# Gate and norm of the decode rows apart from the main rows, and the decode steps spread anew over the projection phase

## The chip, the cores and the metric

The kernel runs on one core of one Trainium2 chip. The metric is the device time of one execution in microseconds; the time of before is the median of three runs. The engines that the text speaks of are TensorE (PE; PEld is its weight load), VectorE (DVE), ScalarE (ACT), GpSimd (POOL) and SyncE (SP), the last of which only issues transfers. ACT and POOL have transfer queues of their own too.

## What is computed

One layer of a decoder, on 1024 prompt positions (the main rows) and 8 decode rows of one position each, side by side as 1032 columns. Cut to the part that the change touches:

```python
proj = rmsnorm(x, norm1_w) @ w_in                 # z (1536) | x, B, C (2048) | dt (24 heads) | v (512)
xbc = silu(causal_dwconv(xbc, conv_state, conv_w, conv_b))
dt = softplus(dt_raw + dt_bias); a = -exp(a_log)
# main rows: the scan over 8 chunks of 128 positions, 24 heads of 64, 4 groups of B and C, state 64
# decode rows, for each head: one step of the same scan
h_new = exp(dt * a) * h + (dt * x) B              # (8 rows, 24, 64, 64): an output
y = sum_n(h_new * C) + d_skip * x
# both kinds of row
y = y * silu(z)
y = rmsnorm over each of 4 groups of 384 channels, times ssd_norm_w
x = x + concat(y, pooling(v)) @ w_out             # then the feed-forward part
```

All values are 32-bit floats. Each large product is made as three TensorE products of high and low parts: weight high with data high, weight high with data low, weight low with data high.

## The kernel before

Channels lie on the 128 partitions, positions along the free axis. `hn` holds eight row blocks of the normed input as high and low parts (`hh`, `hl`). A tile of `w_in` is 128 output channels; `gemm` makes it in three column chunks of 344, 24 products each, into a bank tagged `g`. `load_tile` loads the weights in two halves on SP's queue, and `weight_parts` (L140, L141) lets ACT make the high and a second engine, `lo_eng`, the low half; four half tiles (`wop`) are kept. `lo_eng` is POOL for tiles 1 to 5, 13, 15 and 6 to 9, and DVE from then on.

The order of the projection phase (`project`, `ssd_phase`):

- `startup` loads the input, norms it by column chunk (`norm`) and makes tiles 12 (B of the first two groups), 14 (C) and 0. `norm` lets DVE scale a row block, ACT make its high part and DVE (POOL for some) its low part; the list `low` says how many scaled blocks may wait for their low part. `dt_chain` makes dt, the decay tables of the scan and, for the decode rows, `dtS` (dt of each channel's head by row) and its decay `dA`.
- The tiles of x go through the convolution (`conv_tile`, `conv_close`: one tap on ACT, three on DVE, L516) and get their SiLU one tile later.
- The scan of one half of the heads (6 tiles of x, `q` = 0 and 1: the first and the second group of tasks) is a list of tasks, `queue`, from which `between` takes about two per tile before a column chunk of a running tile. For a chunk `c`, `decay` makes `mix` and `ce` (DVE L538, ACT, then POOL L553), `turn` the transposed inputs (L571 to L583), `apply` the chunk's state `h` (POOL L606, DVE L610) and its output (PE L620 and L630, DVE L638). The second group's tasks run beside gate tiles 0 to 6.
- `gate_tile(i)` makes z of tile i; a later hook, `gate`, has ACT take its SiLU and DVE multiply it in (L698 main rows, L700 decode rows). After each third gate `group_norm` squares and adds, `group_scale` takes the mean over the channels by a product with a matrix of ones (L721), rsqrt as exp(-0.5 ln) on ACT, and scales on DVE (L730).
- `sample_tile(i)` is the decode step of tile i: POOL loads the state `st` and, for some i, B and C broadcast to all partitions (`bc`, L662, from a small DRAM tensor `bcd` that `sample_bc` writes), then makes the new state, stores it, and adds up y over the 64 state entries in six halvings (L680). Its result is written over the tile's x of the decode rows, which L700 waits for.
- Steps 0 to 2 are queued between the two groups, 3 to 6 beside chunks 0, 2, 4 and 6 of the second. Gates 7 to 11, each with its own step ahead of it, come after the scan, and four pooling tiles (`pool_tile`: running sums on DVE L858, `mh` and `ml` as the parts for a small product) end the phase. `w_out` follows, whose first operands are `yh` and `yl`.

`issue_after` (in `behind`) puts an instruction behind another of the same engine; `self.pl` is the last state product L606, behind which the steps beside the scan are put. ACT holds one table set at a time: SiLU is in one set, exp and ln in the other; `tables` chains all such activations in the order of the code and loads a set where it changes. All else is ordered by a scheduler that runs when the program is built: it takes instructions by the order of the code and by when, on its own estimate of the engines' times, their inputs and buffers are there. On the chip each engine then keeps that order.

## Time and profile before

| | us |
|---|---|
| median of 3 runs (lowest, highest) | 1403.73 (1402.88, 1408.87) |
| profiled execution (its span) | 1407.76 (1406.0) |
| PE busy | 1360.4 (97%) |
| DVE, ACT, POOL busy | 991.2, 700.6, 561.5 |

The profile is of one execution. Times are counted from the start of its span. L12 is line 12 of the kernel before. Each row of a timeline gives the start, the length, the engine, line and operation, and in brackets how long the engine stood idle before it and which instruction ended that wait. The granted clock is a share of TensorE's full 2.4 GHz; its lower level, 1.2 GHz, is 0.50. The projection phase lasts until about 516 us, the output projection until about 715 us; the rest is the feed-forward part.

### The profile page before, as it was taken

The page shows a single profiled execution, that of the slowest core. Times are in us where ns is not written, and L with a number is a line of the kernel's source. Part 1 is how long each engine was busy: PE and PEld are TensorE (multiplying, and loading weights), DVE is VectorE, ACT ScalarE, POOL GpSimd, SP SyncE. Part 2 cuts the span into 40 slices and gives each one's busy share as a digit, 9 for nine tenths or more (in the row PEclk, how much of TensorE's full clock was granted, in tenths as well). Part 3 has the DMA queues.
Part 4 walks back from the last instruction along what each step waited for, and adds up shares of the span by engine and source line. Part 5 has one row for each costly group of instructions (what it writes and reads, how often), then busy time and mean ns, then how long its engine had stood idle before and what let it go on. Part 6 is the DMA issues. An engine that isn't in the chain of part 4 may idle for free. (4 is left out here: it accounts for less than half of the span.)

```text
span 1406.0 us, 26779 instructions
## 1 busy us (share of the span) xinstructions
PE 1360.4 (97%) x10360; PEld 1312.9 (93%) x10360; DVE 991.2 (70%) x1453; ACT 700.6 (50%) x1408; POOL 561.5 (40%) x704
## 2 busy tenths in 40 slices
PE   8999999979999999999979999999999999999997
PEld 7799879968799999899979999999999999999997
DVE  6575898669865684844689877777776787567743
ACT  6346774546644451311456545554554465444452
POOL 4233465888668305774222212212222224214122
PEclk9999999989999999999999999999999999999999
DMA  6031235243331256675477877777777769657513
GB/s 248 1 108 38 93 118 168 81 142 116 94 104 62 74 192 209 214 253 178 152 204 148 210 205 193 187 207 183 185 187 201 196 207 328 225 185 235 180 55 121
DMA packets 117820, 228.09 MB, mean 162 GB/s; under 512 B 19884, under 2 KB 37116, under 8 KB 117692
## 3 DMA queue, kind: packets, MB, share of 16 engines
q1 hardware_dynamic: 73772, 130.21, 29.3%
q0 software_dynamic: 27056, 70.22, 19.8%
q10 hardware_dynamic: 16864, 25.95, 5.6%
q8 instruction: 81, 1.33, 0.4%
q14 instruction: 47, 0.39, 0.1%
HBM read 169.64 MB, written 45.15 MB: 153 GB/s over the span
## 5 line engine op out<-in xcount | busy, mean ns | idle before, releaser
L1118 PE MATMUL g<-op,wop 128*128 128x258 f32 x3696 | 446.9, 283 | 4.3 <-DVE op L1048 1.6
L1118 PEld LDWEIGHTS g<-op,wop 128*128 128x128 f32 x3696 | 445.3, 189 | 5.6 <-DVE op L1048 2.0
L140 ACT ACTIVATE wop<-raw 128x512 fp32r<-128x512 f32 (+1 forms) x208 | 125.9, 608 | 231.2 <-PE g L161 139.7
L1300 PE MATMUL g<-op,wop 128*128 128x258 f32 x1848 | 224.9, 283 | 1.6 <-ACT op L210 0.9
L159 PE MATMUL g<-hh,wop 128*128 128x344 f32 x696 | 226.1, 325 | 0.0
L160 PE MATMUL g<-hl,wop 128*128 128x344 f32 x696 | 225.3, 324 | 0.0
L1300 PEld LDWEIGHTS g<-op,wop 128*128 128x128 f32 x1848 | 222.5, 189 | 2.7 <-ACT op L210 1.1
L161 PE MATMUL g<-hh,wop 128*128 128x344 f32 x696 | 224.8, 323 | 0.0
L141 DVE TENSOR_TENSOR wop<-raw,wop 128x512 fp32r<-128x512 f32 (+1 forms) x186 | 159.7, 862 | 83.3 <-ACT wop L140 81.5
L140 ACT ACTIVATE wop<-s 128x512 fp32r<-128x512 f32 (+1 forms) x136 | 83.6, 620 | 137.6 <-PE g L1300 51.9
L1098 POOL DMA_DIRECT2D s<-s x44 | 37.7, 857 | 249.8 <-DVE wop L141 89.2
L159 PEld LDWEIGHTS g<-hh,wop 128*128 128x128 f32 x696 | 132.2, 190 | 1.2 <-issue 1.1
L161 PEld LDWEIGHTS g<-hh,wop 128*128 128x128 f32 x696 | 132.1, 190 | 1.2 <-issue 1.2
L160 PEld LDWEIGHTS g<-hl,wop 128*128 128x128 f32 x696 | 132.1, 190 | 0.5 <-issue 0.4
L1200 DVE SCALAR_TENSOR_TENSOR acc<-u,cst,acc 128x1048 f32<-128x1048 f32 x88 | 115.2, 1309 | 12.2 <-ACT acc L1198 10.6
L141 DVE TENSOR_TENSOR wop<-s,wop 128x512 fp32r<-128x512 f32 (+1 forms) x136 | 92.1, 682 | 36.5 <-ACT wop L140 34.1
L1178 DVE TENSOR_TENSOR u<-u,g 128x258 f32<-128x258 f32 (+2 forms) x176 | 58.0, 354 | 72.2 <-PE g L1118 67.6
L1175 ACT ACTIVATE u<-g 128x258 f32<-128x258 f32 (+2 forms) x220 | 69.6, 340 | 71.2 <-PE g L1118 71.2
L160 PE MATMUL g<-yl,wop 128*128 128x344 f32 x288 | 93.4, 325 | 3.2 <-DVE yl L211 3.2
L161 PE MATMUL g<-yh,wop 128*128 128x344 f32 x288 | 93.0, 323 | 0.0
L159 PE MATMUL g<-yh,wop 128*128 128x344 f32 x288 | 92.9, 323 | 0.0
L1270 POOL DMA_DIRECT2D g<-td x77 | 41.2, 539 | 123.1 <-DVE op L211 70.2
(276 smaller groups left out, 2333.9 us busy)
## 6 DMA issues: line engine op xcount, KB each, us to landing
s<-wup SPq DMA_DIRECT2D x88, 256.0 KB, 3.2
g<-td POOLq DMA_DIRECT2D x77, 258.0 KB, 4.5
raw<-wup SPq DMA_DIRECT2D x66, 256.0 KB, 4.1
raw<-win SPq DMA_DIRECT2D x58, 256.0 KB, 2.7
mix<-acd SPq DMA_DIRECT2D x16, 768.0 KB, 4.5
td<-acc ACTq DMA_DIRECT2D x22, 516.0 KB, 6.1
s<-wup POOLq DMA_DIRECT2D x44, 256.0 KB, 5.3
s<-s POOLq DMA_DIRECT2D x44, 256.0 KB, 3.9
```

The costliest lines, as they stand in the source:

```text
L140: self.nc.scalar.activation(hi, raw[:, :w], AF.Copy)
L141: lo_eng.tensor_tensor(out=lo, in0=raw[:, :w], in1=hi.bitcast(F32), op=ALU.subtract)
L159: nc.tensor.matmul(ps[:, :n], wh, xh[:, sl], start=(first and k == 0), stop=False)
L160: nc.tensor.matmul(ps[:, :n], wh, xl[:, sl], start=False, stop=False)
L161: nc.tensor.matmul(ps[:, :n], wl, xh[:, sl], start=False, stop=(final and k == last))
L1098: nc.gpsimd.dma_start(t, raw[acc] if acc in raw else w[acc][j], accum_op=ALU.add)
L1118: nc.tensor.matmul(out, a, b, start=(p in OPENS and j == 1), stop=(j == 12), skip_group_check=True)
L1175: a = nc.scalar.activation(out, ps[:, s], AF.Copy, scale=-1.0 if p in ("p5", "p4") else 1.0)
L1178: nc.vector.tensor_tensor(out=out, in0=out, in1=ps[:, s], op=op)
L1200: nc.vector.scalar_tensor_tensor(out=acc, in0=u[:, k : k + FW], scalar=self.c("fw", 3 * n + k), in1=acc, op0=ALU.mult, op1=ALU.add)
L1270: self.loaded = self.nc.gpsimd.dma_start(st[:, j], self.td[i + j][ROW[p]]).ins
L1300: self.pe = nc.tensor.matmul(out, a, b, start=(s == 0 and i == 0 and j == 0), stop=(s == len(PIECES) - 1 and i == nk - 1 and j == 2),).ins
```

## The change

- Gate and norm of the decode rows are taken out of `gate`, `group_norm` and `group_scale`, which then handle the 1024 main columns only. ACT puts SiLU of the decode columns of z into a small tile `zs`. A new function, `group_decode(g)`, makes gate, squares, mean (three products with the matrix of ones, 8 columns each) and scale for the decode rows of one group of three tiles. It is called for group 0 after gate tile 9, for group 1 after gate tile 11, for groups 2 and 3 after the last two pooling tiles.
- Decode steps 0 and 1 are made after tiles 1 and 2 of x, ahead of the first group's chunks; steps 2 to 4 beside chunks 2, 4 and 6 of the second group; steps 5 to 8 before gates 7 to 10; steps 9 to 11 after gate 11. The last three take their buffers from the tag `pf`, in pairs. B and C are broadcast for steps 0, 2, 3, 5, 6 and 9 (before: 0, 3, 6, 7 and 9). `sample_bc` is called after tile 1 for the first half, and in the first group's chunk 2 for the second.
- `dtS` comes from a transfer of dt to DRAM and two broadcast loads of it, on POOL's queue, and not from two TensorE products; the matrices for these go from the constants.
- In `norm` of the first column chunk one scaled block may wait for its low part, not two.

```diff
@@ -69,8 +69,8 @@
 NCONST = _n
 
 
-M_ID, M_TRI, M_SEL, M_RM = 0, 128, 256, 384
-NMAT = 384 + 12
+M_ID, M_TRI = 0, 128
+NMAT = 256
 
 
 class Kernel:
@@ -321,7 +321,7 @@
                     if also is not None and k == 0:
                         with self.behind(act):
                             also()
-                    while low and (len(low) > 2 or k == KT - 1):
+                    while low and (len(low) > min(c + 1, 2) or k == KT - 1):
                         j, xj = low.pop(0)
                         hi, lo = self.hn[j]
                         eng = nc.gpsimd if j == 2 or (j == 5 and c > 0) else nc.vector
@@ -411,6 +411,12 @@
         nc.vector.tensor_tensor(out=l, in0=l, in1=q, op=ALU.add)
         self.dt = self.const.tile([P, n9], F32, name="dt")
         nc.vector.scalar_tensor_tensor(out=self.dt, in0=t, scalar=0.0, in1=l, op0=ALU.max, op1=ALU.add)
+
+        dtd = self.dram.tile([NH, NB], F32, name="dtd")
+        nc.gpsimd.dma_start(dtd.rearrange("h b -> b h"), self.dt[:NB, n8:n9])
+        self.dtS = self.const.tile([P, XT, NB], F32, name="dtS")
+        for g in range(2):
+            nc.gpsimd.dma_start(self.dtS[64 * g : 64 * g + 64], dtd[g::2].partition_broadcast(64))
         ea = cut(4 * n9, NH)
         self.tables(ea, self.c("alr", 0, NH), AF.Exp)
         dta = q[:, :n8]
@@ -447,23 +453,6 @@
         nc.sync.dma_start(
             self.acd.rearrange("c (h l) -> h c l", h=NH), rows[:NH, :].rearrange("h (c l) -> h c l", l=P)
         )
-
-        tp = self.bank("pM")
-        nc.tensor.transpose(tp[:NH, :NB], self.dt[:NB, n8:n9], self.mat[:NB, M_ID : M_ID + NB])
-        dts = cut(4 * n9 + NH, NB)
-        nc.vector.tensor_copy(dts[:NH], tp[:NH, :NB])
-        r = cut(900, XT * NB).rearrange("p (i b) -> p i b", b=NB)
-        nc.vector.tensor_tensor(
-            out=r[:NH], in0=self.mat[:NH, M_RM : M_RM + XT].unsqueeze(2).broadcast_to([NH, XT, NB]),
-            in1=dts[:NH].unsqueeze(1).broadcast_to([NH, XT, NB]), op=ALU.mult,
-        )
-        tp = self.bank("pT")
-        nc.tensor.matmul(
-            tp[:, : XT * NB], self.mat[:NH, M_SEL : M_SEL + P], r[:NH].rearrange("h i b -> h (i b)"),
-            start=True, stop=True,
-        )
-        self.dtS = self.const.tile([P, XT, NB], F32, name="dtS")
-        nc.vector.tensor_copy(self.dtS.rearrange("p i b -> p (i b)"), tp[:, : XT * NB])
         ec = cut(1000, XT)
         self.tables(ec, self.c("alc", 0, XT), AF.Exp)
         self.dA = self.const.tile([P, XT, NB], F32, name="dA")
@@ -655,17 +644,20 @@
         nc, d = self.nc, self.d
         g = (i // 3) % 2
         mk = lambda s, shape: self.ph.tile(shape, F32, tag=self.tags[s][0], name=self.nm(s), bufs=self.tags[s][1])
-        if i % 3 == 0 or i == 7:
+        if i % 3 == 0 or i in (2, 5):
             self.bc = mk("bc", [P, 2, NB, NST])
             for j in range(2):
                 src = self.bcd[q : q + 1, :, j * P + g * NST : j * P + (g + 1) * NST]
                 nc.gpsimd.dma_start(self.bc[:, j], src.rearrange("o b n -> (o b) n").partition_broadcast(P))
         bb, cc = self.bc[:, 0], self.bc[:, 1]
         xt = self.xs_samp(self.xs[i])
-        st = mk("st", [P, NB, NST])
+        if self.tags["st"] is None:
+            pair = self.ph.tile([P, 2, NB, NST], F32, tag="pf", name=self.nm("st"), bufs=2)
+            st, tmp = pair[:, 0], pair[:, 1]
+        else:
+            st, tmp = mk("st", [P, NB, NST]), mk("stt", [P, NB, NST])
         nc.gpsimd.dma_start(st, d["st_ssm"][i])
         dx = mk("dx", [P, 2, NB])
-        tmp = mk("stt", [P, NB, NST])
         bcast = lambda a: a.unsqueeze(2).broadcast_to([P, NB, NST])
         nc.gpsimd.tensor_tensor(out=dx[:, 0], in0=self.dtS[:, i, :], in1=xt, op=ALU.mult)
         nc.gpsimd.tensor_tensor(out=tmp, in0=bb, in1=bcast(dx[:, 0]), op=ALU.mult)
@@ -694,10 +686,9 @@
 
         def gate():
             z = box[0]
-            self.tables(z, z, AF.Silu)
+            self.tables(z[:, :SEQ], z[:, :SEQ], AF.Silu)
+            self.tables(self.zs[:, i], z[:, SEQ:TOK], AF.Silu)
             nc.vector.tensor_tensor(out=y[:, :SEQ], in0=y[:, :SEQ], in1=z[:, :SEQ], op=ALU.mult)
-            ys = self.xs_samp(y)
-            nc.vector.tensor_tensor(out=ys, in0=ys, in1=z[:, SEQ:TOK], op=ALU.mult)
             if i % 3 == 2:
                 self.group_norm(i // 3)
 
@@ -706,36 +697,52 @@
 
     def group_norm(self, g):
         nc = self.nc
-        sq = [self.short(SW, "sq") for _ in range(2)]
-        nc.scalar.activation(sq[0], self.xs[3 * g], AF.Square)
+        sq = [self.short(SEQ, "sq") for _ in range(2)]
+        nc.scalar.activation(sq[0], self.xs[3 * g][:, :SEQ], AF.Square)
         for i in range(1, 3):
-            nc.scalar.activation(sq[1], self.xs[3 * g + i], AF.Square)
+            nc.scalar.activation(sq[1], self.xs[3 * g + i][:, :SEQ], AF.Square)
             eng = nc.gpsimd if g < 2 else nc.vector
             eng.tensor_tensor(out=sq[0], in0=sq[0], in1=sq[1], op=ALU.add)
         self.later(2, lambda: self.group_scale(g, sq))
 
     def group_scale(self, g, sq):
         nc = self.nc
-        for j, (o, w) in enumerate(((0, 512), (512, 512), (1024, 32))):
-            pb = self.bank(("pT", "pY")[j % 2])
-            nc.tensor.matmul(pb[:, :w], self.ones, sq[0][:, o : o + w], start=True, stop=True)
-            self.tables(sq[1][:, o : o + w], pb[:, :w], AF.Ln, bias=self.eps, scale=1.0 / 384.0)
+        for j in range(2):
+            pb = self.bank(("pT", "pY")[j])
+            part = slice(j * 512, (j + 1) * 512)
+            nc.tensor.matmul(pb, self.ones, sq[0][:, part], start=True, stop=True)
+            self.tables(sq[1][:, part], pb, AF.Ln, bias=self.eps, scale=1.0 / 384.0)
         self.tables(sq[1], sq[1], AF.Exp, scale=-0.5)
-        for i in range(3):
-            y = self.xs[3 * g + i]
-            for o, a, r in (
-                (y[:, :SEQ], y[:, :SEQ], sq[1][:, :SEQ]),
-                (y[:, SEQ:TOK], self.xs_samp(y), self.xs_samp(sq[1])),
-            ):
-                nc.vector.scalar_tensor_tensor(
-                    out=o, in0=a, scalar=self.c("nw", 3 * g + i), in1=r, op0=ALU.mult, op1=ALU.mult
-                )
+        for i in range(3 * g, 3 * g + 3):
+            y = self.xs[i][:, :SEQ]
+            nc.vector.scalar_tensor_tensor(
+                out=y, in0=y, scalar=self.c("nw", i), in1=sq[1], op0=ALU.mult, op1=ALU.mult
+            )
+
+    def group_decode(self, g):
+
+        nc = self.nc
+        pb = self.bank("pT")
+        for i in range(3 * g, 3 * g + 3):
+            rows, s = self.xs[i][:, SEQ:TOK], self.zs[:, XT + i % 3]
+            nc.vector.tensor_tensor(out=rows, in0=self.xs_samp(self.xs[i]), in1=self.zs[:, i], op=ALU.mult)
+            nc.vector.tensor_tensor(out=s, in0=rows, in1=rows, op=ALU.mult)
+            nc.tensor.matmul(pb[:, :NB], self.ones, s, start=(i % 3 == 0), stop=(i % 3 == 2))
+        r = self.zs[:, XT + 3]
+        self.rsqrt(r, pb[:, :NB], 1.0 / 384.0)
+        for i in range(3 * g, 3 * g + 3):
+            rows = self.xs[i][:, SEQ:TOK]
+            nc.vector.scalar_tensor_tensor(
+                out=rows, in0=rows, scalar=self.c("nw", i), in1=r, op0=ALU.mult, op1=ALU.mult
+            )
 
     def project(self):
 
         nc, d, tc = self.nc, self.d, self.tc
         self.bcd = self.dram.tile([2, NB, 2 * P], F32, name="bcd")
         self.xs, self.bt, self.ctl = [None] * XT, {}, {}
+
+        self.zs = self.const.tile([P, XT + 4, NB], F32, name="zs")
 
         with ExitStack() as outer:
             with self.banks(g=3, pT=2, pY=2, pM=1) as self.ps:
@@ -745,10 +752,17 @@
                     self.ssd_phase()
             with self.banks(g=4, pT=2, pY=1, pM=1) as self.ps, tc.tile_pool(name="mix", bufs=1) as self.ph:
 
-                self.tags = {"bc": ("v", 2), "st": ("mh", 1), "stt": ("ml", 1), "dx": ("vs", 2)}
+                self.tags = {"bc": ("pf", 2), "st": ("mh", 1), "stt": ("ml", 1), "dx": ("vs", 2)}
                 for i in range(7, 12):
+                    if i < 11:
+                        self.sample_tile((i - 2) // 6, i - 2)
+                    self.gate_tile(16 + i, i, None)
+                    if i == 9:
+                        self.group_decode(0)
+                self.group_decode(1)
+                self.tags["st"] = None
+                for i in range(9, 12):
                     self.sample_tile(1, i)
-                    self.gate_tile(16 + i, i, None)
                 self.pool_groups()
 
     def ssd_phase(self):
@@ -784,10 +798,10 @@
                     trn[c + 1] = self.turn(q, c + 1, dec[c + 1][0])
                 if c + 2 < NCH:
                     dec[c + 2] = self.decay(q, c + 2)
-                if c == -1 and q == 0:
-                    self.sample_bc(q)
-                if q == 1 and c in (0, 2, 4, 6):
-                    sample(3 + c // 2)
+                if (q, c) == (0, 2):
+                    self.sample_bc(1)
+                if q == 1 and c in (2, 4, 6):
+                    sample(1 + c // 2)
 
             queue.append(start)
             for c in range(-1, NCH):
@@ -800,15 +814,16 @@
         self.lo_eng = nc.gpsimd
         for n in range(1, 6):
             self.keep(n, self.conv_tile(n, n, None))
+            if n == 1:
+                self.sample_bc(0)
+            if n < 3:
+                sample(n - 1)
         ssd_tasks(0)
         credit[:] = 0.35, 0.6
         for n in (13, 15, 6, 7, 8, 9):
             self.keep(n, self.conv_tile(n, n, between))
         flush()
         self.lo_eng = nc.vector
-        self.sample_bc(1)
-        for i in range(3):
-            queue.append(lambda i=i: sample(i))
         credit[1] = 0.7
         for n in (10, 11):
             self.keep(n, self.conv_tile(n, n, between))
@@ -887,6 +902,8 @@
         pf = {}
         for g in (3, 2, 1, 0):
             pf[g] = self.pool_tile(g, g == 0)
+            if g < 2:
+                self.group_decode(3 - g)
         self.hn = None
         self.w_out([pf[g] for g in range(4)])
 
@@ -1513,8 +1530,6 @@
     s, t = np.arange(P)[:, None], np.arange(P)[None, :]
     m[:, M_ID : M_ID + P] = s == t
     m[:, M_TRI : M_TRI + P] = s <= t
-    m[:, M_SEL : M_SEL + P] = (s % 2) == (t // 64)
-    m[:, M_RM : M_RM + XT] = (s // 2) == np.arange(XT)[None, :]
     return m
 
 
```

## Rows read from the trace of the kernel before

**Rows 1.** The page, first part: busy us of each engine, share, instructions.

```profile
PE 1360.4 (97%) x10360; PEld 1312.9 (93%) x10360; DVE 991.2 (70%) x1453; ACT 700.6 (50%) x1408; POOL 561.5 (40%) x704
```

**Rows 2.** Waits of PE, whole span: us in total, times, longest us.

```profile
PE pY L630 <- POOL ce L553: 9.8, 2, 9.2
...
PE pM L565 <- DVE h L610: 3.7, 4, 1.9
...
PE pY L620 <- DVE mix L583: 2.9, 2, 2.1
...
PE g L160 <- DVE hl L329: 2.6, 2, 2.3
```

**Rows 3.** Stretches: busy us by engine, granted clock, DMA share, GB/s.

```profile
core 0: us, PE busy (x) PEld busy (x) DVE busy (x) ACT busy (x) POOL busy (x), PEclk, DMA share, GB/s
95.00:135.00 40.00, 40.00 (x257) 39.30 (x256) 25.19 (x23) 21.97 (x34) 15.67 (x19) 1.00 0.18 55
...
143.00:219.00 76.00, 71.88 (x644) 61.55 (x641) 73.27 (x104) 52.82 (x116) 45.48 (x33) 0.98 0.37 118
...
310.00:397.00 87.00, 80.69 (x672) 70.15 (x671) 76.64 (x107) 56.16 (x114) 64.76 (x58) 0.96 0.34 109
397.00:471.00 74.00, 74.00 (x458) 72.08 (x458) 39.77 (x39) 35.59 (x52) 60.17 (x81) 1.00 0.26 82
...
471.00:505.00 34.00, 34.00 (x211) 33.01 (x210) 26.04 (x36) 14.75 (x32) 1.02 (x4) 1.00 0.26 74
```

**Rows 4.** Timelines of ACT, POOL and PE round the longest wait.

```profile
279.37 0.83 ACT L188 ACTIVATE ce<-ce 128x768 f32<-128x768 f32 x1
...
280.53 1.84 POOL L662 DMA_DIRECT2D bc<-bcd  x2
...
286.69 1.83 POOL L671 TENSOR_TENSOR stt<-bc,dx 128x512 f32<-128x512 f32 x1 [2.15 <-DMA bc<-bcd]
...
293.24 1.03 POOL L672 TENSOR_TENSOR st<-st,dA 128x512 f32<-128x512 f32 x1 [2.45 <-DMA st<-st_ssm]
294.24 1.79 POOL L553 TENSOR_TENSOR ce<-ce,xs 128x768 f32<-128x768 f32 x1
...
296.08 1.33 PE L630 MATMUL pY<-ce,h 64*64 64x128 f32 x10 [9.19 <-POOL ce L553]
```

**Rows 5.** Stretches of 10 us round that wait, columns as in rows 3.

```profile
290.00:300.00 10.00, 3.92 (x21) 2.82 (x23) 0.86 (x3) 2.00 (x6) 7.41 (x9) 0.50 0.17 52
300.00:310.00 10.00, 10.00 (x72) 9.08 (x69) 8.57 (x13) 1.78 (x4) 9.00 (x13) 0.85 0.51 146
```

**Rows 6.** Timelines of DVE and PE in the first column chunk.

```profile
11.79 2.58 DVE L313 SCALAR_TENSOR_TENSOR x<-x,cst,rs 128x344 f32<-128x344 f32 x3 [1.43 <-ACT rs L188]
14.28 1.57 DVE L329 TENSOR_TENSOR hl<-x,hh 128x344 fp32r<-128x344 f32 x1
...
15.91 0.44 PE L160 MATMUL g<-hl,w0h 128*128 128x344 f32 x1 [2.28 <-DVE hl L329]
```

**Rows 7.** Timelines of POOL, ACT and DVE: three waits.

```profile
76.64 1.29 POOL L141 TENSOR_TENSOR wop<-raw,wop 128x512 fp32r<-128x512 f32 x1 [9.69 <-ACT wop L140]
...
109.95 0.28 ACT L188 ACTIVATE dA<-dA 128x96 f32<-128x96 f32 x1 [3.41 <-DVE dA L470]
...
470.88 0.17 DVE L700 TENSOR_TENSOR xs<-xs,z 128x8 f32<-128x8 f32 x1 [1.95 <-POOL xs L682]
```

**Rows 8.** Timeline of PE: small fp32 products among the large ones.

```profile
103.73 0.32 PE L161 MATMUL g<-hh,wop 128*128 128x344 f32 x1
103.88 0.32 PE L159 MATMUL g<-hh,wop 128*128 128x344 f32 x1
104.13 0.46 PE L461 MATMUL pT<-dtw,mat 24*128 24x96 f32 x2
104.52 0.43 PE L160 MATMUL g<-hl,wop 128*128 128x344 f32 x1
...
475.34 0.30 PE L721 MATMUL pT<-sq,ones 128*128 128x32 f32 x2
475.48 0.40 PE L161 MATMUL g<-hh,wop 128*128 128x344 f32 x1
```

**Rows 9.** DVE's low halves: those from 397 to 471, and one alone.

```profile
L141 DVE TENSOR_TENSOR wop<-raw,wop 128x512 fp32r<-128x512 f32 x12 | 12.9, 1080 | 18.3 <-ACT wop L140 18.2
...
477.16 0.69 DVE L141 TENSOR_TENSOR wop<-raw,wop 128x512 fp32r<-128x512 f32 x1 [0.23 <-ACT wop L140]
```

**Rows 10.** ACT's table loads: count, ns min/median/max.

```profile
L181 ACT ACT_TABLE_LOAD  x29: 1283/1283/1283, 0.7 to 1168.6; - x29
```

**Rows 11.** Timelines of DVE and PE at the first pooling product; first product of `w_out`.

```profile
491.20 1.23 DVE L211 TENSOR_TENSOR ml<-sa,mh 128x1032 fp32r<-128x1032 f32 x1 [0.27 <-ACT mh L210]
...
496.69 0.32 PE L160 MATMUL pT<-ml,pw 128*128 128x344 f32 x1
...
515.87 0.32 PE L159 MATMUL g<-yh,wop 128*128 128x344 f32 x1
```

**Rows 12.** DVE and POOL side by side at 578; `yl` of 505 to 520.

```profile
578.19 11.96 DVE L211 TENSOR_TENSOR yl<-xs,yh 128x1032 fp32r<-128x1032 f32 x4
...
579.17 4.54 POOL L1253 TENSOR_TENSOR ds<-ds,ds 128x512 f32<-128x512 f32 x2
...
L211 DVE TENSOR_TENSOR yl<-xs,yh 128x1032 fp32r<-128x1032 f32 x6 | 7.2, 1228 | 1.1 <-ACT yh L210 1.1
```

## The prediction

> **What bounds the kernel now.** I read the page's first part first: TensorE (PE) is busy 1360.4 of 1406.0 us [rows 1], so only the 46 us in which it stands idle, what its lower clock costs after such a stand, and the number of its instructions can move the time. Vector (DVE), Scalar (ACT) and GpSimd (POOL) matter where PE waits for them. Next come the waits of PE. Four of those that this change touches lie in the projection phase: 9.8 us for POOL's `ce` (the longest single one 9.2), 3.7 for DVE's `h`, 2.9 for `mix`, 2.6 for `hl` [rows 2]. Then I cut the span into the stages of the code [rows 3]. Beside the first group's chunks (143 to 219) PE is idle 4.1 us and DVE is busy 73.3 of 76; beside the second group's (310 to 397) PE is idle 6.3 and DVE busy 76.6 of 87; beside the last gates (397 to 471) and the pooling tiles behind them (471 to 505) PE never stands.
>
> The one large stall has a clear history [rows 4]. ACT ended the exponential of the second `ce` at 280.2 us. POOL's product with C, 1.8 us long, started only at 294.24, because POOL's program has decode steps 2 and 3 in front of it: it issued the broadcast loads of B and C, waited 2.15 us for them, issued the state load and waited 2.45 us for that. PE waited until 296.08. The fast clock went with it: 0.50 granted over 290 to 300 and 0.85 over 300 to 310 [rows 5], and 0.50 is 1.2 GHz. Of the 3.92 and 10.00 busy us there, 2.0 and 1.5 would not have been needed at 2.4 GHz. The stall costs 9.2 + 3.5 = 12.7 us, or 1.38 us for each idle one; I use that factor for other long stands.
>
> **The change part by part.**
>
> *Fewer decode steps before and beside the second group (7 to 3).* Steps 0 to 2 no longer stand between the groups, and the step that was issued with chunk 0 is gone; what put them in front of `ce` was that this step waits only for the first group's last state update. The first one that is left comes with chunk 2, and is held behind that chunk's state product on POOL. At 280 us POOL then has nothing but `ce` and `h` to do. I take the stall as gone: -12.7 (0 if POOL's order puts another step there). The steps beside chunks 2, 4 and 6 stay as many as before at those places, so the other 6.3 idle us of the stage stay in my sum; they could shrink by up to 6.3 x 1.38 = 8.7, since the main gates no longer wait for a step on DVE.
>
> *Startup.* In the first column chunk DVE now makes the low half of row block 0 after two scaled blocks instead of three. The three took 2.58 us, so it starts 0.9 earlier, and PE, which waited 2.28 us for it, starts 0.9 earlier [rows 6]. -0.9; between 0 (the next block is late instead) and -2.3.
>
> *The decode dt through DRAM.* A transpose, a copy, a product, a select matmul and a copy go; three DMAs on POOL's queue come, the two loads behind the store. POOL is idle for 9.7 us ahead of the weight half at 76.6 us [rows 7], so their waits cost nothing there; if the three chained transfers took more than that, the halves of a later tile would wait, of which four are kept ahead. The decay `dA` is late today, its exponential ends at 110.2 [rows 7], and ACT's SiLUs of the first tiles follow it in ACT's order; they come earlier. PE was not waiting there: 0.
>
> *Matmuls.* Twelve 8-column fp32 matmuls (two passes each) come, four of 32 columns and the select pair go. The select pair moved the next product from 0.16 to 0.64 us behind the one before it, so it cost 0.48; the 32-column pair right behind others of the same weights cost 0.14 [rows 8]. Twelve at 0.14 to 0.48, taken at 0.30 since two DVE steps lie between them but their weights are alike: 3.6 (1.7 to 5.8). Minus four at 0.14 and 0.48: +2.5 (0.6 to 4.8).
>
> *Two decode steps ahead of the chunks (tiles 1 to 5).* Five steps took POOL from 397 to 471, so one is 14.8 us of wall time, 12.0 of it busy [rows 3]. Two make 29.6 us inside the 40 from 95 to 135, where POOL was busy 15.7 and DVE 25.2. POOL also makes the low weight halves there, some 17 us before they are needed (three buffers of half a tile; a tile's 72 products at 0.16 us make 11.7 us), so their delay is covered. What isn't free is DVE: beside decode steps its 512-column subtraction took 1.08 us on average, alone 0.69 [rows 9], a factor 1.57. On 25.2 x 29.6/40 = 18.6 us of DVE work that makes 10.6 more, against 14.8 idle. I take +1 (0 to 10.6 x 1.38 = 14.6): the stage behind has 2.7 us of spare DVE time and passes on what is left.
>
> *Seven steps beside the last gates (5 before), gate and norm of decode rows apart.* DVE loses its waits for a step (1.95 us before the gate of tile 11 [rows 7]); the small products (8 columns) are about as many as before and lie in idle DVE time: 0. Two more table loads on ACT (1.28 us each [rows 10]), one pair round the decode norm of group 1, lie where ACT is busy 35.6 of 74: 0; without that cover 2.6. Steps 5 to 11 end near 397 + 7 x 14.8 = 501 plus one more pair of broadcast loads, some 503. The decode norm of group 3 waits for the last of them; the output projection starts at 516 [rows 11], so 13 us cover that wait, with everything DVE and PE have queued behind it. But from 471 to 505 POOL was idle and DVE busy 26.0 of 34, and now 2.3 steps lie there. With the factor 1.57 DVE needs 14.8 more against 8.0 idle: 6.8 late. PE took the low half `ml` of the pooling product 4.2 us after it was ready [rows 11], so 2.6 reach PE, 3.6 with the clock. I take +2 (0 to 3.6 by that row, more in the rivals).
>
> Two rows show DVE and POOL at their worst together [rows 12]: four `yl` subtractions beside POOL's additions took 11.96 us, alone 1.23 each. That is 7.0 us more, while POOL was at work for all of them. The Trainium skill ("SBUF — State Buffer", section "SBUF: two separate sides") calls the port pair that the two share an exclusive lock: a GpSimd instruction, or a DVE one with two SBUF inputs, keeps the other out for its whole length. These rows agree with it. By that rule POOL's whole busy time, not a factor on DVE's, would be the price of a step; that is the third and the second rival below.
>
> Sum: -12.7 - 0.9 + 2.5 + 1 + 2 = -8.1 us. The profiled execution took 1407.8 us (span 1406.0 and 1.8 around it), so it would have taken 1399.7. It lies 4.0 above the median of the three runs, 1403.7; the median becomes 1395.7.
>
> **Rivals.**
> 1. *The wait stays.* The scheduler may again put a decode step in front of a `ce` (the three left, each with its DMA waits). For it: steps 2 and 3 both carry a broadcast load now. Against: with chunks 2, 4 and 6 of before PE waited only 0.6 us for `ce` in all (9.8 less 9.2). Time: 1395.7 + 12.7, less what a shorter one saves, 1402 to 1408.
> 2. *The pooling tiles become DVE's.* POOL's busy time, 2.3 x 12.0 = 27.7, and DVE's 26.0 make 53.7 in 34 us if they take turns: up to 19.7 late. With half of that, 10, PE waits (10 - 4.2) x 1.38 = 8 instead of 2: 1401.7. Against it: in 397 to 471 the two were busy 100 us in 74 and PE never stood.
> 3. *Slower: the first group starts late.* Steps 0 and 1 lie right ahead of its chunks. If they fall on busy DVE stretches (the taps of tiles 4 and 5), DVE is up to 24 us late at 143, and from there to 219 it has 2.7 us to spare, so nearly all of it reaches PE. At 14 us late the time is 1394.7 + 14 x 1.38 = 1414; it decides from (1410.7 - 1394.7)/1.38 = 11.6 us on. For it: 73.3 busy of 76 [rows 3]. Against it: DVE is idle 14.8 us from 95 to 135.
>
> **How the numbers follow.** Less than 0.5%, 7 us, can't be told from no change here: faster means below 1396.7, slower above 1410.7. Forecast, 0.56, its own range 1389 to 1400: 0.46 of it faster, 0.10 within. Rival 1, 0.11: 0.01, 0.09 and 0.01 slower. Rival 2, 0.16: 0.01 faster, 0.15 within. Rival 3, 0.17: 0.02 within, 0.15 slower. In all 0.48, 0.36, 0.16. The range 1386 to 1411 takes in the forecast with 8.7 us for the second group's other stalls, rivals 1 and 2 and the small end of rival 3; it leaves out most of rival 3.
>
> **What would show it.** Right: no PE wait for `ce` over 1 us, a granted clock near 1.0 where the second group starts, POOL's steps 5 to 11 ending near 503 less what was gained, PE idle under 3 us from the last gate to the output projection. Wrong: a `ce` behind a decode step again; PE waits for `ml` or `yl` beside steps 9 to 11; DVE late at the first chunks, with PE waits for `h` or `mix` above the 3.7 us there.

## The result, and the profile after

The changed kernel is slower: median 1415.4 us against 1409.1 for before, 14 executions of each; ratio 1.0048 (95%: 1.0026 to 1.0069), so +6.7 us (6.3 between the medians) where -8.1 was forecast. The forecast of 1395.7 counted from 1403.7, the median of three executions; over 14 of them before stands 5.4 us higher. The profiled execution took 1417.5 us.

Part 1 of its page answers to [rows 1]: PE is busy 8 us longer, and the span is 9.7 longer.

```profile
PE 1368.3 (97%) x10373; PEld 1317.6 (93%) x10373; DVE 983.9 (69%) x1462; ACT 705.0 (50%) x1426; POOL 561.9 (40%) x709
```

The waits of PE answer to [rows 2]. The forecast stall has gone (`ce`, now L542, 1.0 us instead of 9.8), but two waits for `h`, and waits for `u`, `wop` and `sq`, are there instead.

```profile
PE pM L554 <- DVE h L599: 7.3, 2, 3.7
...
PE g L159 <- ACT u L490: 2.4, 1, 2.4
...
PE g L161 <- POOL wop L141: 1.8, 1, 1.8
PE pT L713 <- DVE sq L705: 1.7, 1, 1.7
PE g L159 <- ACT u L493: 1.6, 1, 1.6
PE pY L619 <- POOL ce L542: 1.0, 1, 1.0
```

This table is worked out from windows of 2 us, each row from one profiled execution: idle is the stretch less PE's busy time, clock is busy time times (1 - granted clock), and the rest of the stretch is work. Tiles 1 to 5 run from the first product of tile 1 to the first state product of the scan, the first group from there to its last state product, the second group from its first to its last state product, and the last gates with the pooling tiles from there to the first product with `yh`. Each of these cells is the loss, idle + clock. The work column counts the whole stretch up to the feed-forward part, with the startup, the tiles between the groups and the output projection; the last column is the end of that stretch.

```
                       tiles 1-5  1st group  2nd group  last gates,  work to     feed-forward
                                                        pooling      feed-fwd    starts at
before                    0.0        5.6       22.0        0.0         672.1       717.7
changed                   8.9        6.4       13.6        2.6         678.3       728.6
changed, second (E12)     7.3        7.0       10.0        3.0         678.5       722.7
E4  changed, dA later     0.0        8.0        7.5        2.8         678.5       715.0
E13 changed, old dt       2.5        6.5       12.6        8.0         681.3       725.3
E5  steps 0, 1 early      2.8        5.9       13.5        0.1         673.5       714.2
E14 gate apart alone      0.0        5.8       20.2        0.0         677.1       721.2
E15 fastest               0.0        7.8       10.0        2.3         672.1       706.6
```

The second group's loss fell by 8.4 us. Its start runs at the full clock, but past 310 us PE waits again, for `h`, as it does early in the first group. DVE makes both `h` (L599), and in the first group three taps (multiply-adds of the convolution) stand ahead of it. They took 2.2 us each beside a busy POOL; the tap at 171.61, with POOL idle, took 1.30 (line numbers are each kernel's own):

```profile
290.00:300.00 10.00, 10.00 (x80) 8.17 (x81) 10.00 (x19) 6.68 (x16) 1.26 (x2) 1.00 0.39 133
300.00:310.00 10.00, 10.00 (x85) 9.36 (x83) 10.00 (x15) 5.64 (x15) 8.30 (x8) 1.00 0.78 198
310.00:320.00 10.00, 6.38 (x61) 5.52 (x58) 8.30 (x14) 7.08 (x17) 9.12 (x8) 0.71 0.51 182
```

```profile
162.66 6.56 DVE L505 SCALAR_TENSOR_TENSOR xs<-u,cst,xs 128x1056 f32<-128x1056 f32 x3
169.14 0.54 DVE L599 TENSOR_TENSOR h<-h,pM 128x384 f32<-128x384 f32 x1
...
171.61 1.30 DVE L505 SCALAR_TENSOR_TENSOR xs<-u,cst,xs 128x1056 f32<-128x1056 f32 x1
...
169.74 0.33 PE L554 MATMUL pM<-mat,xs 128*128 128x128 f32 x1 [3.72 <-DVE h L599]
...
315.39 0.48 PE L554 MATMUL pM<-mat,xs 128*128 128x128 f32 x1 [3.62 <-DVE h L599]
```

Tiles 1 to 5, where the prediction wrote 0 for dt and +1 for the two steps, lost 8.9; PE's work grew by 6.2. Most of that loss is a chain through four engines' orders. First the stretches (columns as in [rows 3]), then POOL, DVE, ACT and PE in the changed kernel:

```profile
80.00:90.00 10.00, 8.45 (x54) 8.16 (x54) 0.26 (x1) 3.72 (x7) 3.95 (x5) 1.00 0.45 32
90.00:100.00 10.00, 7.62 (x39) 7.33 (x38) 9.40 (x7) 6.92 (x11) 3.73 (x3) 0.83 0.50 155
130.00:140.00 10.00, 8.23 (x43) 7.95 (x42) 6.61 (x3) 3.02 (x6) 9.82 (x10) 0.83 0.22 79
```

```profile
71.05 0.75 POOL L416 DMA_DIRECT2D dtd<-dt  x1 [2.90 <-DVE dt L413]
78.82 1.52 POOL L419 DMA_DIRECT2D dtS<-dtd  x2 [7.03 <-DMA dtd<-dt]
...
85.96 0.26 DVE L459 SCALAR_TENSOR_TENSOR dA<-dtS,dtw 128x96 f32<-128x96 f32 x1 [8.11 <-DMA dtS<-dtd]
90.60 2.55 DVE L505 SCALAR_TENSOR_TENSOR xs<-u,cst,xs 128x1056 f32<-128x1056 f32 x2 [4.38 <-ACT xs L503]
...
86.25 0.28 ACT L188 ACTIVATE dA<-dA 128x96 f32<-128x96 f32 x1 [8.69 <-DVE dA L459]
86.55 1.28 ACT L181 ACT_TABLE_LOAD   x1
87.85 0.45 ACT L492 ACTIVATE u<-g 128x336 f32<-128x336 f32 x1
...
88.43 0.42 PE L159 MATMUL g<-hh,wop 128*128 128x344 f32 x1 [1.55 <-ACT u L493]
94.84 0.43 PE L159 MATMUL g<-hh,wop 128*128 128x344 f32 x1 [2.38 <-ACT u L490]
```

The reader is to see one small instruction holding two engines. The store of dt lets POOL go on only 7.03 us later; the loads then take until 85.96. DVE's `dA` (0.26 us of work) holds up DVE's order for 8.11 us, and the exponential of `dA` holds up ACT's for 8.69. Behind these two stand the evacuation `u` of a finished bank (the copy out of it, without which PE can't use it again) and the first convolution tap, which reads ACT's L503. DVE is busy 0.26 us of ten. PE runs out of free banks, waits twice, and is granted a mean clock of 0.83 over the next ten us: the lower level for about a third of them, by the two levels of 1.00 and 0.50.

A third wait lies later, at 133 us: 1.8 for POOL's low weight half (`wop`), while POOL, with decode steps and weight halves to make, is busy 9.82 us of ten. With the clock it makes the rest of the 8.9. The trace of E1 below, with the late dt but without the early steps, lacks this wait and loses 5.5 here; that of E4, with the early steps but without the late `dA`, loses nothing. So this part needs both.

### The profile page after: what moved, and what is told of

It reads as the page before. It is cut to its first block, busy times and chain, and to the rows that moved or that the text cites. A ratio compares the mean times of both kernels' runs of the same rounds, so it can differ in the third digit from the quotient of the medians.

```text
span 1415.7 us, 26829 instructions
## 1 busy us (share of the span) xinstructions
PE 1368.3 (97%) x10373; PEld 1317.6 (93%) x10373; DVE 983.9 (69%) x1462; ACT 705.0 (50%) x1426; POOL 561.9 (40%) x709
## 4 chain that ended last, share of the span: by engine, by line
PE 72%; DVE 11%; POOL 7%; DMA 5%; issue 3%; ACT 2%; DVEq 0%; SPq 0%; POOLq 0%; ACTq 0%
PE g L1135 30%; PE g L1317 16%; PE g L160 7%; PE g L161 7%; PE g L159 7%; DMA ds<-wdn 1%; DVE xs L505 1%; DVE wop L141 1%; DVE mix L527 1%; DVE mix L572 1%; POOL st L672 1%; POOL ds L1270 1%; PE pY L609 1%; DMA st<-st_ssm 1%; DVE xs L627 1%
## 5 line engine op out<-in xcount | busy, mean ns | idle before, releaser
L141 DVE TENSOR_TENSOR wop<-raw,wop 128x512 fp32r<-128x512 f32 (+1 forms) x186 | 156.1, 843 | 78.3 <-ACT wop L140 76.3
```

What stands on the lines that cost most here:

```text
L141: lo_eng.tensor_tensor(out=lo, in0=raw[:, :w], in1=hi.bitcast(F32), op=ALU.subtract)
```

## The experiments

Ratios are to the kernel before on the same chip, with their 95% interval. 0.1% is 1.4 us. Twelve executions stand behind each, eleven behind E13 and six behind E3 and E9; E8 and E12 are one execution each, for a trace. A trace is of one execution and need not be a typical one.

**E1**, before with dt through DRAM alone:

```diff
+        nc.gpsimd.dma_start(dtd.rearrange("h b -> b h"), self.dt[:NB, n8:n9])
+        for g in range(2):
+            nc.gpsimd.dma_start(self.dtS[64 * g : 64 * g + 64], dtd[g::2].partition_broadcast(64))
-        nc.tensor.transpose(tp[:NH, :NB], self.dt[:NB, n8:n9], self.mat[:NB, M_ID : M_ID + NB])
...
-        nc.vector.tensor_copy(self.dtS.rearrange("p i b -> p (i b)"), tp[:, : XT * NB])
```

> The kernel before, with one part of the change alone: the decode dt goes through DRAM (one store, two broadcast loads), the transpose, select product and their copies are gone; the steps stay where they were. Theory A (the queue behind the wait): the decay dA stands on DVE right ahead of the convolution taps and on ACT ahead of an evacuation; DVE waits some 8 us for the second load (in the changed kernel 8.11 of 15 us of transfers), the first tap slips from 80.9 to about 90, PE waits 3 to 6 us near 88 and 95 and its clock drops to 0.5 for one or two slices: 5 to 9 us slower than before, no PE wait of this size from 66 to 105 in the trace of before. Rival B (the loss belongs to decode steps 0 and 1 beside the taps, the prediction's rival 3): dA late hurts nobody, within 1.5 us of before. Rival C (prediction): 0, or 0.5 faster for the products that are gone.

Ratio 1.0054 (1.0032 to 1.0076): +7.6 us, as theory A said, with the same DVE wait and the same two stretches. The trace is of the slowest of the twelve (1421.3): tiles 1 to 5 lose 5.5 where before loses nothing, and the first scan product comes at 150.1 instead of 142.3; the second group loses 28.9 in it (before 22.0).

```profile
85.58 0.26 DVE L459 SCALAR_TENSOR_TENSOR dA<-dtS,dtw 128x96 f32<-128x96 f32 x1 [8.10 <-DMA dtS<-dtd]
```

```profile
80.00:90.00 10.00, 8.46 (x54) 8.18 (x53) 0.26 (x1) 4.10 (x7) 2.73 (x3) 1.00 0.40 31
90.00:100.00 10.00, 7.63 (x39) 7.35 (x38) 9.78 (x8) 6.93 (x12) 3.45 (x2) 0.83 0.54 169
```

**E4**, the changed kernel with `dA` and its exponential taken out of `dt_chain` into `decode_decay`; the transfers stay:

```diff
             if n == 1:
+                self.decode_decay()
                 self.sample_bc(0)
```

> The changed kernel, with the three transfers left as they are and only the two instructions of dA (DVE product, ACT exponential) issued after tile 1. It tells the transfers from what is queued behind the instruction that waits for them. Theory A: nothing on DVE or ACT stands behind the transfers any more, so as much is won as by making dt on TensorE: 5 to 9 us faster than the changed kernel; the store and the loads take their 15 us as before. Rival B (the transfers hold POOL's queue, and with it the low weight halves): PE still waits near 88, 95 and 133, under 2 us faster. Rival C (steps 0 and 1 are the cause): under 2 us faster, no waits near 88 and 95, the same delay by 151.

Ratio 1.0002 (0.9982 to 1.0022), 6.5 us better than the changed kernel's 1.0048. The transfers take as long as in the changed kernel (POOL waits 7.06 for the store), but DVE and ACT no longer wait for them, and PE's ten-us stretches are full:

```profile
78.70 1.52 POOL L419 DMA_DIRECT2D dtS<-dtd  x2 [7.06 <-DMA dtd<-dt]
...
104.56 0.23 DVE L462 SCALAR_TENSOR_TENSOR dA<-dtS,ec 128x96 f32<-128x96 f32 x1
```

```profile
80.00:90.00 10.00, 10.00 (x65) 10.00 (x64) 8.62 (x6) 6.67 (x9) 3.63 (x5) 1.00 0.73 111
90.00:100.00 10.00, 10.00 (x66) 9.86 (x65) 10.00 (x7) 4.71 (x7) 4.93 (x3) 1.00 0.77 247
```

So it is the place of the waiting instruction in its engine's order, not the transfers, that costs. The change as a whole is still no faster than before: +0.3 us, between -2.5 and +3.1.

**E3**, the changed kernel with the old dt, and **E9**, before with gate and norm apart; in both the select matrices came into the startup's memory, for want of room:

```diff
+            self.sel = sp.tile([P, NSEL], F32, name="sel")
+            nc.sync.dma_start(self.sel, d["mat"][:, NMAT:])
```

> The changed kernel, with the decode dt made by the two TensorE products again (the select matrices have no room among the constants beside zs, so they lie in the startup's own memory and come by a transfer of their own). Theory A (the queue behind the wait): the 8.1 us wait on DVE goes, PE waits near 88 and 95 and the low clock there go: 5 to 9 us faster than the changed kernel, so 1 to 4 us faster than before. Rival B (steps 0 and 1 beside the taps are the cause): 0 to 2 us faster than the changed kernel, PE still late by 7 to 9 us at the first scan product (151).

> The kernel before with gate and norm of the decode rows apart (twelve 8-column products, four 32-column ones gone) and nothing else: the steps, dt and the startup order as before. (The two select matrices lie in the startup's own memory, with a transfer of their own, since there is no room beside zs.) Theory A (the products stand on PE's path at 0.51 each, less four of about 0.4): PE's work up to the feed-forward part 4 to 6 us over the 672.1 of before, loss beside the second group about the 22 of before, since its stall stays: 3 to 6 us slower than before. Rival B (the prediction's 2.5): 2 to 3 us slower. Rival C (the main gates, which no longer wait for a step on DVE, win it back beside the second group): not slower.

E3: 1.0081 (1.0057 to 1.0105); E9: 1.0124 (1.0092 to 1.0155). Both missed every theory, by the same fault of my own edit: with the matrices in that memory, the two products come right behind the transposes in PE's order, not among the next tiles' products, and PE itself takes the waits (tiles 1 to 5 lose 15.9 and 14.9; with the matrices among the constants, in E13 and E14, 2.5 and 0.0). In E3:

```profile
82.79 0.18 PE L455 MATMUL pM<-mat,dt 8*24 8x8 f32 x1 [4.46 <-ACT rows L449]
90.26 0.73 PE L464 MATMUL pT<-dtw,sel 24*128 24x96 f32 x2 [7.29 <-DVE dtw L459]
```

Neither counts for its question; E13 and E14 ask again.

**E13**, the changed kernel with the old dt, the matrices among the constants (squares and scale of the decode norm in used places of `dtS` and `dA`, which frees the room):

```diff
-            rows, s = self.xs[i][:, SEQ:TOK], self.zs[:, XT + i % 3]
+            rows, s = self.xs[i][:, SEQ:TOK], self.dtS[:, i]
-        r = self.zs[:, XT + 3]
+        r = self.dA[:, 3 * g]
```

> The changed kernel with dt by products again; the select matrices lie among the constants as in before, for which squares and scale of the decode norm use the places of dtS and dA that are done with. Theory A (the wait for the transfers cost 8 to 9 us, the rest of the change nearly nothing): 6 to 9 us faster than the changed kernel, at the level of before; tiles 1 to 5 lose 0 to 3 us as in E5 (2.8). Rival B (steps 0 and 1 cost in the changed kernel what they did not cost in E5): less than 4 faster, with PE late by 149 or more at the first scan product (142 in before, 146 in E5).

Tiles 1 to 5 behaved as said (2.5, table), but the time did not: 1.0078 (1.0053 to 1.0102), no faster than the changed kernel's 1.0048, so theory A missed in time. In its trace most of the gain is given back at the last gates (8.0, where the changed kernel has 2.6) and in work (681.3 against 678.3). The main norm's addition L716 stands on DVE behind a decode row's gate L739, which waits for POOL's decode step:

```profile
477.48 0.17 DVE L739 TENSOR_TENSOR xs<-xs,zs 128x8 f32<-128x8 f32 x1 [6.36 <-POOL xs L685]
477.68 1.47 DVE L740 TENSOR_TENSOR dtS<-xs 128x8 f32<-128x8 f32 x1
479.07 1.21 DVE L716 TENSOR_TENSOR sq<-sq,sq 128x1024 f32<-128x1024 f32 x1
```

```profile
480.33 2.07 PE L724 MATMUL pT<-sq,ones 128*128 128x512 f32 x2 [4.25 <-DVE sq L716]
```

The changed kernel has the same order there and loses 1.65 us by it (L728 at 481.88 waits 6.36, L705 is next). The profiled execution, 1414.4 us, is one of the fastest of E13; what makes its times worse than E4's by 0.8% stays open beyond this wait.

**E14**, before with gate and norm apart, clean (`group_decode` and the shortened gate and norm as in the change, rooms as in E13):

> The kernel before with gate and norm of the decode rows apart and nothing else, the select matrices among the constants. Theory A (twelve products at 0.3 to 0.5 us, less four 32-column ones): 4 to 6 us more PE work up to the feed-forward part than the 672 of before, 3 to 6 us slower than before. Rival B (the prediction): 2.5. Rival C (won back beside the second group, where the main gates no longer wait for a step): not slower.

Ratio 1.0012 (0.9984 to 1.0039). PE's work is 677.1, +5.0 as theory A has it; the second group lost 1.8 less in this trace, though its `ce` stall stays (8.9 us). In time that is +1.7, between -2.2 and +5.5: not told from nothing, so the time doesn't choose between the theories.

**E6** adds the squares of a group on DVE, so that one product stands for three, on top of E4; **E7** is E6 with the old startup order:

```diff
+        for k in (1, 2):
+            nc.vector.tensor_tensor(out=s, in0=s, in1=self.zs[:, XT + k], op=ALU.add)
+        nc.tensor.matmul(pb[:, :NB], self.ones, s, start=True, stop=True)
```

```diff
-                    while low and (len(low) > min(c + 1, 2) or k == KT - 1):
+                    while low and (len(low) > 2 or k == KT - 1):
```

> The changed kernel with dA later, and in the decode norm the three squares of a group added on DVE, so that one product with the ones stands where three stood: 8 of 12 products (16 of 24 passes) go. In the trace a pass takes 256 ns, so a product 0.51, and PE's work at full clock grew by 6.2 us from before to after up to the feed-forward part. Theory A (a product costs its 0.51 us, the prediction's upper end): 16 x 0.256 = 4.1 us less work, 3 to 5 us faster than the kernel with dA later. Rival B (the prediction's 0.30 each): 2.4 us. Rival C (they hide under the loads of weights, 0.14 each): 1 us; the growth then comes from elsewhere.

> The kernel of the run before (dA later, one product per group), with the old order of scaled blocks and low parts in the first column chunk. Its time tells little (under 1 us expected); read in the trace where the first product of tile 1 stands: 65.6 to 65.9 with the old order in three traces, 66.1 and 66.2 with the new one. Theory A (the new order only shifts the start: PE waits less for the first low part and as long for the next ones): 65.6 to 65.9, so 0.2 to 0.6 us gained. Rival B (the prediction: 0.9 gained by the new order): 67.0. With E6 this should be the fastest of all: 5 to 8 us faster than before.

E6: 1.0015 (0.9997 to 1.0034), not faster than E4, where 3 to 5 us were expected. The work did fall as theory A has it, by 4.0 us up to the feed-forward part (678.5 to 674.5), 3.0 of it from the last gates on. But PE lost 14.7 beside the second group (E4 7.5) and 5.4 at the last gates (2.8). E7, with the same norm, lost 10.3 and 5.6: the second group's part changes from one execution to the next, the last gates' part came twice. E7: 1.0015 (0.9996 to 1.0033), the first product of tile 1 at 65.5, in E6 at 65.7: the startup edit is worth nothing that can be read, and neither is the fastest of all, as had been expected.

**E2** and **E8** (the same program twice), before with step 3 beside chunk 1:

```diff
-                if q == 1 and c in (0, 2, 4, 6):
+                if q == 1 and c in (1, 2, 4, 6):
```

> The kernel before, with decode step 3 issued beside chunk 1 of the second group and not beside chunk 0; nothing else. Theory A: the 9.2 us wait for ce at 287 to 296 goes, as POOL has no load in front of that ce; but part of the gain is given back, because in the stage of the second group DVE is busy 77 of 87 us and PE meets other waits there (h, mix): 3 to 9 us faster than before. Rival B (the prediction's term): the whole 12.7 us, idle and clock. Rival C: the wait moves to the next ce or h, behind the same loads: under 2 us.

> The kernel with step 3 beside chunk 1 once more, for a second trace. Its twelve times fell into two heaps, 1399.5 to 1402.1 and 1407.4 to 1412.3; the trace read was of the lower one. Theory A: if this execution falls into the upper heap, its stages show where the 6 to 8 us lie: a place that waits for a transfer, so that the same program does or doesn't meet a wait. Rival B: the loss is spread evenly over the clock. If it falls into the lower heap again, it says how far the stages repeat.

Ratio 0.9995 (0.9973 to 1.0017): nothing gained that can be told, under theory A's 3 to 9. E2's trace has no `ce` wait and loses 14.0 beside the second group. E8's loses 20.3: PE waits 4.2 for a `ce` and 9.63 for `sq`. E8's time, 1406.2 on another chip, lies between E2's two heaps. The two programs are the same; POOL at the same instruction, E2's lines first, then E8's:

```profile
290.80 1.04 POOL L672 TENSOR_TENSOR st<-st,dA 128x512 f32<-128x512 f32 x1 [0.82 <-DMA st<-st_ssm]
...
292.76 1.29 POOL L673 TENSOR_TENSOR stt<-st,stt 128x512 f32<-128x512 f32 x1
294.01 2.57 POOL L553 TENSOR_TENSOR ce<-ce,xs 128x768 f32<-128x768 f32 x1
...
293.13 1.73 DVE L583 TENSOR_TENSOR mix<-mix,cb 128x768 f32<-128x768 f32 x1
294.79 2.61 DVE L578 TENSOR_TENSOR xd<-xd,wd 128x768 f32<-128x768 f32 x1
```

```profile
294.02 6.52 POOL L672 TENSOR_TENSOR st<-st,dA 128x512 f32<-128x512 f32 x1 [0.89 <-DMA st<-st_ssm]
...
294.09 0.94 DVE L583 TENSOR_TENSOR mix<-mix,cb 128x768 f32<-128x768 f32 x1
294.96 0.95 DVE L578 TENSOR_TENSOR xd<-xd,wd 128x768 f32<-128x768 f32 x1
...
341.34 2.65 POOL L672 TENSOR_TENSOR st<-st,dA 128x512 f32<-128x512 f32 x1 [4.74 <-DMA st<-st_ssm]
...
351.33 2.34 PE L721 MATMUL pT<-sq,ones 128*128 128x512 f32 x4 [9.63 <-POOL sq L714]
```

In E2 POOL's product is done, in 1.04 us, before DVE's two operations start; these then meet POOL's next two instructions, and both engines are stretched. In E8 DVE runs unstretched and POOL's product takes 6.52. `ce` is behind it; and 50 us later `sq` stands behind a state load that POOL waits 4.74 us for (2.23 in E2). So the same stage meets other waits in another execution of the same program; what decides between them is not shown.

**E5** and **E16** (again, another chip), before with steps 0 and 1 after tiles 1 and 2:

```diff
+            if n == 1:
+                self.sample_bc(0)
+            if n < 3:
+                sample(n - 1)
...
-        for i in range(3):
+        for i in range(2, 3):
             queue.append(lambda i=i: sample(i))
```

> The kernel before, with decode steps 0 and 1 made after tiles 1 and 2 of x (as in the changed kernel) and only step 2 left between the groups; dt by TensorE products, step 3 beside chunk 0. It asks what the two steps ahead of the chunks cost by themselves, without the wait for the transfers of dt. Theory A (the transfers with their queue did the harm, the steps little): 0 to 2.5 us of PE loss from 66 to 142, where the kernel before has 0; beside the first group 5 to 9 us, where it has 5.6; no slower than 4 us in all. Rival B (the prediction's rival 3, DVE late at the first chunks): 8 us or more of new loss up to 228. Rival C: the products that spread dt are drawn ahead in PE's order, as the steps need them early, and PE waits for them some 10 us near 85, as in the changed kernel with the old dt.

> E5 once more on another chip. Theory A: its gain of 5 us (ratio 0.9964) belongs to the program: 3 to 7 us faster than before, loss beside the second group 10 to 15. Rival B (it was a lucky set of twelve runs; the stage beside the second group falls now one way and now the other): 0 to 2 us, and a loss there near 20.

Ratios 0.9964 (0.9947 to 0.9982) and 0.9968 (0.9945 to 0.9991): about 5 us faster, twice. The longest `ce` wait is 2.2 and 1.8 us, though step 3 is still beside chunk 0: with one step between the groups, not three, POOL is through with it at 275.3 in E5, before the `ce` of 284.7. The first group lost 5.9 and 8.4 (before 5.6), tiles 1 to 5 2.8 and 4.6, and the second group 13.5 and 6.3 (before 22.0), the latter under the 10 to 15 expected of E16.

**E10** is E5 with E2's edit; **E11** is E10 and **E15** is E5, each with dt through DRAM and `dA` later:

The diffs are those above.

> The kernel before with steps 0 and 1 after tiles 1 and 2 (E5) and step 3 beside chunk 1 (E2). E5 alone was 5 us faster than before, its loss beside the second group 13.5 where before has 22.0. Theory A (both edits take away the same stall, so they don't add): 0 to 2 us from E5, that is 4 to 7 faster than before. Rival B (they add): 8 to 11 faster.

> The kernel of the run before, with dt through DRAM and dA made after tile 1. In E5 the products that spread dt cost PE 2.8 us of waits and its tiles 1 to 5 took 80.1 us; in the changed kernel with dA later that stretch took 75.4 without a wait. Theory A (the transfers are good once nothing stands behind them): 3 to 5 us faster than the run before, 8 to 11 us faster than before, the fastest of all. Rival B (what is won there is waited for at the first chunks, as in the changed kernel with dA later, where they lost 8.0 against 5.9): 1 to 3 us faster than the run before.

> E5 (before with steps 0 and 1 after tiles 1 and 2) with dt through DRAM and dA after tile 1; gates, norm and startup as before, step 3 beside chunk 0. Theory A: tiles 1 to 5 take 75.4 us without a wait instead of 80.1, and half of it is given back at the first chunks as in E11: 1 to 4 us faster than E5 beside it. Rival B: all of it is given back, within 1 us of E5.

E10: 0.9988 (0.9969 to 1.0007), no better than E5; the edits don't add, and the time falls short of theory A's 4 to 7 us. E11: 0.9978 (0.9955 to 1.0000), 3 us faster than before, not 8 to 11: its tiles 1 to 5 lose nothing, as expected, but the time goes with rival B. E15: 0.9954 (0.9930 to 0.9978), 1401.4 against 1407.0, the fastest of all and ahead of both kernels; that it beats E5 (E16, 1402.2 beside it) is not shown, which is rival B.

**E12**, the changed kernel again:

> The changed kernel once more, for a second trace. Theory A (the wait for the transfers of dt belongs to the program): the stretch from tile 1 to the first scan product loses 8 to 10 us again (8.9 in the first trace), with DVE waiting about 8 us for the loads of dt. The waits beside the second group (13.6) may come out otherwise, between 7 and 17, as the program with step 3 later had 14.0 and 20.3 there in its two traces. Rival B (the first trace was an accident): the first stretch loses under 4.

Its first stretch lost 7.3, under the 8 to 10 of theory A but far above rival B's 4; DVE's `dA` waited 7.24 us, and PE waited 3.0 us for POOL's `wop` and 3.1 for `u`. The wait belongs to the program.

## Why the prediction was wrong

The step that failed is *The decode dt through DRAM*, costed at 0: "POOL is idle for 9.7 us ahead of the weight half at 76.6 us [rows 7], so their waits cost nothing there [...] PE was not waiting there: 0". It looked at the queue that issues the transfers and not at the engines that wait for them. It even wrote that `dA` "is late today" and that what follows it comes earlier: `dA` did come earlier, its exponential at 86.25 instead of 109.95 [rows 7], and thereby ahead of the taps and the evacuations. E1 (+7.6) and E4 (6.5 back) agree on its price; E13 confirms it in the trace of tiles 1 to 5, not in time.

This is about half of the 14.8 us between -8.1 and +6.7. Without it, in E4, the change stands at +0.3, and the other half lies in the terms below: above all the `ce` stall, the largest term, was credited with 12.7 us, and the products with half of their cost.

The signs that the prediction named for being right nearly all came: `ce` 1.0, the clock 1.00, the last step by 494, PE idle 2.6 at the end of the phase. They watched the parts that had a price; none watched the part put at 0.

The other terms, against the runs:

- *The ce stall, -12.7.* It went (1.0), and the granted clock over 290 to 310 was 1.00, where [rows 5] have 0.50 and 0.85. But the stage's loss fell by 8.4 in one trace and 12.0 in the other, and new waits for `h` stand in the first (3.62 at 315.39); the term counted a stall and not its stage. Taken away alone (E2) it brought nothing that can be measured: -0.7 us, between -3.8 and +2.4.
- *Matmuls, +2.5.* The direction was right, the size half: a pass of the 8-column product took 256 ns in the middle (172 at the least), so a product 0.51, just above the bounds of 0.14 to 0.48 and not the 0.30 taken. Work grew by 5.0 in E14, and fell by 4.0 in E6, where 8 products went.
- *Two steps ahead of the chunks, +1, and rival 3.* Moving the steps alone makes the kernel 5 us faster (E5, E16). Where they now lie, in tiles 1 to 5 and the first group, 3.1 and 7.4 us more were lost, above the +1 but within its range; the second group lost 8.5 and 15.6 less. Where the first group was late (first scan product at 151.2 instead of 142.3), it was late by dt: 150.1 in E1 without early steps, 141.5 in E4 with them. Rival 3 gave nearly the right time, 1414, by the wrong cause; that is luck.
- *Seven steps beside the last gates, +2.* 2.6 and 3.0, near the number, but not by `ml`: 1.65 and 2.1 of it come by the order on DVE, where the gate of a decode row waits 6.36 us for POOL ahead of a main row's addition, and 0.8 by a wait for ACT. The prediction had "DVE loses its waits for a step"; the data dependence went, the place in the order stayed. Over the span DVE stood 32.3 us, in eight waits, ahead of the decode rows' gates (L728), in before 3.9 in two (L700). The last step ended at 494, before the 503 forecast.
- *Startup, -0.9.* PE's one wait of 2.28 [rows 6] became two of 0.79 and 0.73, and tile 1 started at 66.2 and 65.7 (before 65.6): 0.
- *Rivals 1 and 2* did not occur.

First trace against first, from the start to the feed-forward part, in us: +8.9 (tiles 1 to 5) + 6.2 (work) + 2.6 (last gates) + 1.0 (between the groups) + 0.8 (first group) - 8.4 (second group) - 0.2 (startup and output projection) = 10.9, which is 728.6 less 717.7. The feed-forward part was 1.2 shorter.

## What to carry to other kernels

Cost a new wait at the engine that waits: read what stands behind the waiting instruction in that engine's order and who needs it, and do the same for instructions that an edit makes ready earlier, since they move ahead. Splitting data apart doesn't free an engine while both parts stay in its order, one behind the other. When a stall is taken away in a stage whose engines are nearly full, don't credit the whole stall: other waits of the stage can take its place. Read a second trace of the same program before believing the first.

## What the runs showed of the hardware

- The store of 192 values of 4 bytes to DRAM held POOL for 7.03 us (7.06 in E4, 6.78 in E1), and the two broadcast loads (64 partitions of 96 values each) were there 5.6 us after they had been issued (80.34 to 85.96). The Trainium skill ("DMA: Bandwidth & Descriptors", section "Rules for kernel authors") says that a strided last dimension becomes one descriptor per element; the same page ("Anatomy of one DMA — SWDGE (gpsimd) path") gives about 2.0 us fixed per transfer. An estimate by that figure for three transfers in a row, 6.0 us, is less than half of what this trace shows from 71 to 86. The trace shows no time for the single elements: it has 32 packets for the store, all between 72.25 and 72.75, and then none but one packet of instructions until the loads are issued at 78.8. What the 6 us between are spent on is not shown.
- A POOL product that took 1.04 us in E2 took 6.52 in another execution of the same program (E8). There six two-input operations of DVE in a row, from 294.09 to 299.65, ran at their short times beside it (the first in 0.94), and it ended 0.9 us behind the last. In E2 the first two of them took 1.73 and 2.61 beside POOL's next two instructions. The Trainium skill ("SBUF — State Buffer", section "SBUF: two separate sides") calls the port pair of the two an exclusive lock that goes to the one that starts first, for its whole instruction. Both traces agree with a lock, with either engine as the loser, but in E8 POOL stayed out over six instructions, not one. E2's times fell into 1399.5 to 1402.1 and 1407.4 to 1412.3; that the lock parts these two heaps is argued from two traces, not shown.
